# RWKV in a hybrid trunk layer: Gram products of two heads in turn, wider group spacing, other buffer counts, split weights kept in DRAM

## The chip, the core and the metric

The kernel runs on one core of a Trainium2 chip. The core has a matrix engine (TensorE, PE in the profile, with PEld for its weight loads), three engines for element work (VectorE, DVE; ScalarE, ACT; GpSimd, POOL) and a queue engine (SyncE, SP) that issues the transfers between DRAM and the on-chip memory. The engines run side by side, each in the order of its own instruction list, and wait for each other through semaphores. Matrix products land in PSUM, eight banks of 128 partitions by 512 fp32 numbers; everything else on chip is in SBUF. The metric is the device time of one execution in microseconds.

## What is computed

One layer over 2048 positions of width 1024. The normalised input goes through one input projection (1024 to 4224 columns), whose columns feed three groups: an RWKV-7 group of eight heads of 64, an S5 group and an RG-LRU group. Each group's output is gated; the concatenation goes through an output projection, and a per-layer embedding is added. Cut to what matters here:

```python
xn = rmsnorm(h, norm_g)
zin = xn @ w_in                          # 1024 x 4224
z_rw, g_rw, u_s5, g_s5, x_lru, g_lru = jnp.split(zin, SPLITS, axis=-1)
# RWKV: token shift, decay d, kk = k / |k|, b = kk * a, and per head
def step(S, inp):
    r_t, k_t, v_t, kk_t, b_t, d_t = inp
    S = S * d_t - (S kk_t) b_t^T + v_t k_t^T
    return S, S r_t
y = group_norm(y) * ln_w + ln_b + bonus;  y_rw = y * silu(g_rw)
h = h + concat(y_rw, y_s5, y_lru) @ w_out
h = h + rmsnorm(p @ ple_w) * sigmoid(h @ ple_gate_w)
out = rmsnorm(h)
```

## The kernel before

**Stages.** First comes one long stretch with the input projection, RWKV and RG-LRU; then the S5 group with the first output products between its steps (`o1a`), then S5's gating (`glu`), then the embedding and the end (`stage_a`, `stage_b`). The first stretch works on two halves of 1024 positions, each in two blocks of 512.

**Projection (`fills`).** 33 panels of 128 columns of `w_in`. `fetch_w` loads a panel as two pieces of 256 KB; `split_w` (L188) writes it as a rounded part `whi` (ACT, L192) and the rest `wlo` (DVE, L193, by the helper at L80), two buffers each; `inproj` (L327) runs 24 products per block: `whi` and `wlo` with the rounded input, `whi` with the input's rest. Both halves load and split all panels. `more()` starts the next panel whenever one is taken. In front of each half, `load_xn` transposes the normalised input rows on TensorE (L319); the rows of the second half are loaded into SBUF buffers that RWKV uses too (`XT`, among them `bk`, `ms`, `kb` and `gr`).

**RWKV.** 16 units, each two head pairs' worth of 256 positions in eight chunks of 64; partitions 0 to 63 hold one head, 64 to 127 the other. Each unit goes through three stages:

- `rwkv_front` (L376): decay and scaling; `kx` (queries and keys, three sets of columns), `bk`; then the Gram products of keys with queries (L461), for each half of the chunks and each head four products of 64 rows by 128 columns into one PSUM bank (`pprep`, two banks, also used by others); ACT copies parts of the bank to `mt` (L466), DVE multiplies the masks into `kx` and `gr` (L468).
- `rwkv_solve` (L471): DVE solves the 32 x 32 triangular blocks in 31 steps (L484 to L489), transposes the result to `tn` and then, in four pieces of 32 partitions, into `tm` (L497); TensorE transposes `bk` into `kb` (L504); small products fill the off-diagonal block of `tm` (L530 from `mt` and `tn`, L541).
- `rwkv_chain` (L549): four steps of state recurrence with products L570, L581, L585 (reads `tm`), L592 and L603, each step three ticks; then the group norm (L608 to L619).

**Order.** TensorE's order is written by hand, by the loop at L879 to L903. Each round is a tick: the projection gets a credit of 10 (9 after the first eight units), a k-step of three products costs 3; then chain, solve and front run up to their next `yield`, whose value says after how many ticks they go on. `W_BK` is the wait between `kx`/`bk` and the Gram, `yield 1` stands before each Gram group, `W_SOLVE` = 8 stands before L530, and a front starts at least 15 ticks (`INTERVAL`) after the one before. A front waits at L428 until the unit two before it has left the chain; `kx`, `gr`, `mt` and `tm` have two buffers. The other engines' orders, and SP's, come from a planner that places each instruction by priority and by when its plan has the inputs ready; the on-chip space of a later stage is that of ended ones, and each later tile waits for the last reader of what lay there.

**After the stretch.** L976 to L981 load `w_out` in rows of 512 KB through three staging buffers (`ht`), round them on ACT (L105) and subtract on DVE; L1008 transposes a small S5 table; `o1a(0)` (L958 to L966) uses the `w_out` rows in the order in which they come.

Of the kernel before, what the change touches and what calls it, by code (L numbers as in the profile page):

```python
# [9 lines left out]
F32 = mybir.dt.float32  # L10
# [7 lines left out]
P = 128  # L18
# [4 lines left out]
C = 64  # L23
# [2 lines left out]
TU = TB // 2  # L26
CHUNK_MM, INTERVAL = (10, 9), 15
PR_C, PR_S, PR_F, PR_W = 100, 50, 0, 0
W_LOAD, W_Z, W_BK, W_SOLVE, W_GN, W_C = 2, 1, 3, 8, 1, 1
K_LATE = (3, 5)  # L30
KD = D // P
CT = W // P
# [12 lines left out]
def hymba_layer(ctx: ExitStack, tc: tile.TileContext, x, p, norm_g, w_in,  # L45
# [20 lines left out]
    Ud = dram.tile([W, T5, NC5], F32, name="Ud")  # L66
    Gd = dram.tile([CT, P, SEQ], F32, name="Gd")
    Zd = dram.tile([W, T5, NC5], F32, name="Zd")

    def pmm(bufs=3):  # L70
        return psum.tile([P, 512], F32, tag="mm", name="ps_mm", bufs=bufs)

    def pprep():
        return psum.tile([P, 512], F32, tag="prep", name="ps_prep", bufs=2)

    def plate():
        return psum.tile([P, 512], F32, tag="late", name="ps_late", bufs=1)
# [4 lines left out]
    def mul(out, a, b):  # L82
        tt(out, a, b, ALU.mult)
# [4 lines left out]
    def sub(out, a, b):  # L88
        tt(out, a, b, ALU.subtract)

    def ts(out, a, s1, op0, s2=None, op1=None):
        if op1 is None:
            V.tensor_scalar(out=out, in0=a, scalar1=s1, scalar2=None, op0=op0)  # L93
        else:
            V.tensor_scalar(out=out, in0=a, scalar1=s1, scalar2=s2, op0=op0, op1=op1)
# [89 lines left out]
            nc.sync.dma_start(out=raws[-1], in_=w_v[:, ks, c0:c0 + P])  # L185
        return raws

    def split_w(raws):  # L188
        hi = wpool.tile([P, KD, P], F32R, tag="whi", name="whi", bufs=2)
        lo = wpool.tile([P, KD, P], F32R, tag="wlo", name="wlo", bufs=2)  # L190
        for ks, raw in zip(w_halves, raws):
            A.copy(out=hi[:, ks], in_=raw)  # L192
            sub(lo[:, ks], raw, hi.bitcast(F32)[:, ks])  # L193
        return hi, lo

    rows, off = [], {}
# [179 lines left out]
    def rwkv_front(pair, z, n):  # L376
# [48 lines left out]
        nc.sync.dma_start(out=inv, in_=nd.rearrange("h b c t -> (h b c) t").unsqueeze(1).broadcast_to([32, 4, 32]))  # L425
        ts(inv, inv, 1e-24, ALU.max)
        V.reciprocal(out=inv, in_=inv)
        while len(chained) < n - 1:  # L428
            yield 0
        kx = wt("kx", [P, NCH, 3, C], 2)  # L430
        mul(kx[:, :, 2], ch(r), ep[:, :, 1:C + 1])
        mul(kx[:, :, 0], ch(kk), ep[:, :, 0:C])
        A.copy(out=kx[64:128, :, 1], in_=kx[64:128, :, 0])
# [13 lines left out]
            stt(r[:, cs], r[:, cs], col("r_k", hp), km[:, cs], ALU.mult, ALU.mult)  # L447
        yield W_BK

        gr = wt("gr", [P, NCH, 2, C], 2)  # L450
        mt = wt("mt", [P, NCH, C], 2)
        for half_c in range(2):
            yield 1
            cs = slice(4 * half_c, 4 * half_c + 4)
            for h in range(2):
                os = slice(64 * (1 - h), 64 * (1 - h) + 64)
                ps = pprep()
                for q in range(4):
                    c = 4 * half_c + q
                    hs = slice(64 * h, 64 * h + 64)  # L460
                    T.matmul(out=ps[:, q * P:(q + 1) * P], lhsT=bk[hs, c].rearrange("p a t -> p (a t)"),  # L461
                             rhs=kx[hs, c, h:3:2 - h], start=True, stop=True)
                psq4 = ps.rearrange("p (c t) -> p c t", t=P)
                for bl in range(2):
                    g = slice(64 * h + 32 * bl, 64 * h + 32 * bl + 32)
                    A.copy(out=mt[g, cs, 0:C - 32 * bl], in_=psq4[g, :, 32 * bl:C])  # L466
                for dst, rs, o in ((kx[os, cs, h], os, 0), (gr[:, cs, h], slice(0, P), C)):
                    mul(dst, psq4[rs, :, o:o + C], gm[rs, o:o + C].unsqueeze(1).broadcast_to([dst.shape[0], 4, C]))  # L468
        return kx, gr, mt, inv, bk, r, dl

    def rwkv_solve(n, v, mt, inv, bk, r):  # L471
        def wt(tag, shape=None, bufs=1):
            return pool_of(tag).tile(shape, F32, tag=tag, name=tag, bufs=bufs)
# [8 lines left out]
        for o, n in ((0, 16), (16, 15)):  # L482
            mul(ms[:, o:o + n, o + 1:32], ms[:, o:o + n, o + 1:32], inv[:, o + 1:32].unsqueeze(1).broadcast_to([P, n, 31 - o]))
        for st in range(31):  # L484
            ni, n = st // 4 + 1, 31 - st
            tmp = wt("stmp", [P, 8, 32], 2)
            mul(tmp[:, 0:ni, 0:n], xs[:, 0:ni, st:st + 1].broadcast_to([P, ni, n]),
                ms[:, st:st + 1, st + 1:32].broadcast_to([P, ni, n]))
            sub(xs[:, 0:ni, st + 1:32], xs[:, 0:ni, st + 1:32], tmp[:, 0:ni, 0:n])  # L489
        tn = wt("stmp", [P, 8, 32], 2).rearrange("p i (c q) -> p i c q", q=4)  # L490
        V.transpose(out=tn.rearrange("p i c q -> p i (c q)"), in_=xs)
        tm = wt("tm", [P, NCH, C], 2)
        for h in range(2):
            G.memset(tm[64 * h + 32:64 * h + 64, :, 0:32], 0.0)
            for bl in range(2):
                g = slice(64 * h + 32 * bl, 64 * h + 32 * bl + 32)
                V.transpose(out=tm[g, :, 32 * bl:32 * bl + 32], in_=tn[g].rearrange("p i c q -> p c i q"))  # L497

        kb = wt("kb", [P, NCH, P], 2)
        for q in range(2):  # L500
# [26 lines left out]
        for c in range(NCH):  # L527
            for h in range(2):
                o = 64 * h
                T.matmul(out=psc[o + 32:o + 64, 32 * c:32 * c + 32], lhsT=mt[o:o + 32, c, 32:64],  # L530
                         rhs=tn[o:o + 32, :, c], start=True, stop=True, tile_position=(o, o + 32))
        qn = wt("stmp", [P, 8, 32], 2)
        for h in range(2):
            hs = slice(64 * h + 32, 64 * h + 64)
            A.copy(out=qn[hs], in_=psc[hs, 0:256].rearrange("p (c t) -> p c t", t=32))
        yield 1
        psd = plate()
        for c in range(NCH):
            for h in range(2):
# [9 lines left out]
    def rwkv_chain(pair, half, q, q_, gd):  # L549
# [15 lines left out]
        for st in range(NS):  # L565
# [162 lines left out]
    def fills(half, xt, w, prev):  # L728
# [7 lines left out]
        raws, ws = [w], []  # L736
# [91 lines left out]
    fronts, begun, solved, chained, ended = [], [], [], [], []  # L828

    def need(*key):  # L830
        while key not in done:
# [301 lines left out]
    def wt(tag, shape, bufs=1):  # L1133
        return sw.tile(shape, F32, tag=tag, name=tag, bufs=bufs)
# [280 lines left out]
```

## Time and profile before

| what | us |
|---|---|
| median of three runs | 1819.96 |
| the three runs | 1819.87 to 1821.08 |
| the profiled execution, its own time | 1823.06 |
| its span, first to last instruction | 1821.3 |
| TensorE busy in the span | 1747.5 |
| VectorE busy | 1287.9 |
| ScalarE busy | 968.8 |

The stretch with RWKV and the projection runs from the start to about 1157 us. In the rows of a stretch, "(x3624)" is the number of instructions, and the clock column is the share of TensorE's full clock that was granted (0.989 over the span). A row of a timeline begins with its start and its length in us; "[4.99 <-DMA st]" says that the engine stood idle for 4.99 us before it and what ended that. Rows with the same line in sequence are merged, with their count. A row of a group ends with total busy us and the mean of one in ns, then the idle time before such instructions. Every fp32 product stands as two rows in the trace (512 rows at L461 for 256 products), a transpose as one.

### The profile page before, as it was taken

How to read it: one execution, taken by the hardware profiler on the slowest of the kernel's cores; microseconds unless marked ns; L12 is line 12 of the kernel's file. 1: busy time of each engine (PE TensorE's matmuls, PEld its weight loads, DVE VectorE, ACT ScalarE, POOL GpSimd, SP SyncE). 2: the span in 40 equal slices, each digit the busy share in tenths (PEclk: the TensorE clock that was granted, in tenths of full speed). 3: DMA queues.
4: the chain of work that ended last, by engine and by line, in shares of the span. 5: the costliest groups of instructions: out<-in, count | busy, mean ns of one | idle time of the engine just before them, and what ended most of it. 6: DMA issues, size and time to landing. Idle time of an engine off the chain costs nothing. (4 is left out here: it accounts for less than half of the span.)

```text
span 1821.3 us, 30173 instructions
## 1 busy us (share of the span) xinstructions
PE 1747.5 (96%) x11212; PEld 1346.6 (74%) x11212; DVE 1287.9 (71%) x3219; ACT 968.8 (53%) x1857; POOL 43.7 (2%) x105
## 2 busy tenths in 40 slices
PE   5999999999998999999999999899999999999997
PEld 4877777777676777777776767678888778888886
DVE  6279788688887439888688885786875685555554
ACT  5345864575757445665558565666763452232222
POOL 1000000000000000000000000000000000000000
PEclk9999999999999999999999999999999999999999
DMA  4332323222223233123222121742334893223220
GB/s 147 116 108 79 93 78 99 90 61 77 83 71 100 82 116 112 52 86 101 82 80 67 51 69 38 197 142 98 110 105 119 221 311 143 85 92 110 78 73 35
DMA packets 214620, 184.71 MB, mean 101 GB/s; under 512 B 59253, under 2 KB 182474, under 8 KB 214474
## 3 DMA queue, kind: packets, MB, share of 16 engines
q1 hardware_dynamic: 214474, 182.79, 32.5%
q8 instruction: 88, 1.44, 0.3%
q14 instruction: 58, 0.48, 0.1%
HBM read 121.73 MB, written 59.83 MB: 100 GB/s over the span
## 5 line engine op out<-in xcount | busy, mean ns | idle before, releaser
L332 PE MATMUL ps_mm<-xh,whi 128*128 128x512 f32 x1056 | 463.0, 438 | 0.9 <-ACT whi L192 0.7
L333 PE MATMUL ps_mm<-xh,wlo 128*128 128x512 f32 x1056 | 416.3, 394 | 0.8 <-DVE wlo L80 0.8
L334 PE MATMUL ps_mm<-xl,whi 128*128 128x512 f32 x1056 | 416.5, 394 | 0.0
L332 PEld LDWEIGHTS ps_mm<-xh,whi 128*128 128x128 f32 x1056 | 200.0, 189 | 79.1 <-issue 31.3
L333 PEld LDWEIGHTS ps_mm<-xh,wlo 128*128 128x128 f32 x1056 | 200.6, 190 | 46.6 <-issue 13.0
L334 PEld LDWEIGHTS ps_mm<-xl,whi 128*128 128x128 f32 x1056 | 200.0, 189 | 45.2
L80 DVE TENSOR_TENSOR stmp<-xs,ms 128x60 f32<-128x60 f32 (+24 forms) x496 | 103.3, 208 | 11.6
L80 DVE TENSOR_TENSOR xs<-xs,stmp 128x60 f32<-128x60 f32 (+24 forms) x496 | 102.7, 207 | 11.5
L923 PE MATMUL ps_mm<-woh,yl 128*128 128x512 f32 x256 | 103.1, 403 | 2.0 <-DVE yl L98 2.0
L922 PE MATMUL ps_mm<-woh,yh 128*128 128x512 f32 x256 | 102.4, 402 | 0.5 <-ACT yh L101 0.4
L924 PE MATMUL ps_mm<-pgl,hh 128*128 128x512 f32 x256 | 101.1, 395 | 0.3 <-DVE pgl L80 0.3
L924 PE MATMUL ps_mm<-wol,yh 128*128 128x512 f32 x256 | 101.3, 396 | 0.0
L923 PE MATMUL ps_mm<-pgh,hl 128*128 128x512 f32 x256 | 101.0, 394 | 0.0
L922 PE MATMUL ps_mm<-pgh,hh 128*128 128x512 f32 x256 | 100.8, 394 | 0.0
L80 DVE TENSOR_TENSOR wlo<-wraw,whi 128x512 fp32r<-128x512 f32 x132 | 88.5, 683 | 14.0 <-ACT whi L192 13.6
L101 ACT ACT_TABLE_LOAD x74 | 94.9, 1283 | 1.3
L101 ACT ACTIVATE ftg<-ps_mm 128x512 f32<-128x512 f32 x32 | 19.1, 598 | 135.4 <-PE ps_mm L924 135.4
L98 DVE SCALAR_TENSOR_TENSOR z<-ps_mm,pc,z 128x511 f32<-128x511 f32 x48 | 35.8, 745 | 69.9 <-ACT z L101 69.8
L192 ACT CAST whi<-wraw 128x512 fp32r<-128x512 f32 x132 | 77.9, 614 | 0.7 <-DMA wraw<-in_w_in 0.2
L98 DVE SCALAR_TENSOR_TENSOR e<-ftg,e 128x1024 f32<-128x1024 f32 x16 | 19.6, 1226 | 78.1 <-ACT ftg L101 78.1
L101 ACT ACTIVATE uv<-ps_chain 64x128 f32<-64x128 f32 x64 | 17.4, 272 | 97.9 <-DVE uv L93 97.2
L101 ACT ACTIVATE z<-ps_mm,dc 128x512 f32<-128x512 f32 x48 | 32.8, 682 | 66.3 <-PE ps_mm L334 66.2
(332 smaller groups left out, 3535.9 us busy)
## 6 DMA issues: line engine op xcount, KB each, us to landing
wraw<-in_w_in SPq DMA_DIRECT2D x132, 256.0 KB
zd<-z SPq DMA_DIRECT2D x48, 256.0 KB
yr<-Yd SPq DMA_DIRECT2D x16, 512.0 KB
Hd<-ht SPq DMA_DIRECT2D x16, 512.0 KB
hr<-Hd SPq DMA_DIRECT2D x16, 512.0 KB
xr<-in_x SPq DMA_DIRECT2D x16, 512.0 KB
out<-e SPq DMA_DIRECT2D x16, 512.0 KB
st<-in_w_out SPq DMA_DIRECT2D x12, 512.0 KB
```

What stands on the lines that cost most here:

```text
L80: V.tensor_tensor(out=out, in0=a, in1=b, op=op)
L98: V.scalar_tensor_tensor(out=out, in0=a, scalar=s, in1=b, op0=op0, op1=op1)
L101: A.activation(out=out, in_=in_, func=func, scale=scale, bias=bias)
L192: A.copy(out=hi[:, ks], in_=raw)
L332: T.matmul(out=ps, lhsT=hi[:, k], rhs=xh, start=(k == 0), stop=False)
L333: T.matmul(out=ps, lhsT=lo[:, k], rhs=xh, start=False, stop=False)
L334: T.matmul(out=ps, lhsT=hi[:, k], rhs=xl, start=False, stop=(k == KD - 1))
L922: T.matmul(out=ps, lhsT=a_h[:, k], rhs=b_h[k][:, ns], start=(ends[0] and k == 0), stop=False)
L923: T.matmul(out=ps, lhsT=a_l[:, k], rhs=b_h[k][:, ns], start=False, stop=False)
L924: T.matmul(out=ps, lhsT=a_h[:, k], rhs=b_l[k][:, ns], start=False, stop=(ends[1] and k == nk - 1))
```

## The change

- **Gram.** The two heads' products are issued in turn, chunk by chunk, into two banks taken together, and both banks are read afterwards. The first group comes one tick after the wait, the second three ticks after the first (`W_GR`); `W_BK` goes from 3 to 4.
- **Waits of the order.** `kx` has three buffers, and the front waits for the chain of three units before it there; before the Gram it waits for the chain of two units before it and for L530 of the unit before (`coupled`). `mt` and `tm` have one buffer; L541's products wait in the order until the last L585 of the unit before is issued (`used`).
- **Transposes into `tm`.** Two of 128 partitions instead of four of 32; the two memsets of POOL that zero a block come after them.
- **Weights.** In the first half `split_w` also stores both parts of each panel to DRAM (`Wd`); in the second half `load_w` loads these into the `whi` and `wlo` buffers, and nothing is fetched or split there.

```diff
-W_LOAD, W_Z, W_BK, W_SOLVE, W_GN, W_C = 2, 1, 3, 8, 1, 1
+W_LOAD, W_Z, W_BK, W_GR, W_SOLVE, W_GN, W_C = 2, 1, 4, (1, 3), 8, 1, 1
+    Wd = dram.tile([w_in.shape[2] // P, 2, P, KD, P], F32, name="Wd")
...
+    def load_w(j):
+
+        pair = w_pair()
+        for i, part in enumerate(pair):
+            nc.sync.dma_start(out=part.bitcast(F32), in_=Wd[j, i])
+        return pair
...
             sub(lo[:, ks], raw, hi.bitcast(F32)[:, ks])
+        for i, part in enumerate((hi, lo)):
+            nc.sync.dma_start(out=Wd[j, i], in_=part.bitcast(F32))
         return hi, lo
...
-        while len(chained) < n - 1:
+        while len(chained) < n - 2:
             yield 0
-        kx = wt("kx", [P, NCH, 3, C], 2)
+        kx = wt("kx", [P, NCH, 3, C], 3)
...
+        while len(chained) < n - 1 or len(coupled) < n:
+            yield 0
         gr = wt("gr", [P, NCH, 2, C], 2)
-        mt = wt("mt", [P, NCH, C], 2)
+        mt = wt("mt", [P, NCH, C])
         for half_c in range(2):
-            yield 1
+            yield W_GR[half_c]
             cs = slice(4 * half_c, 4 * half_c + 4)
+            pair_ps = [pprep(), pprep()]
+
+            for q in range(4):
+                c = 4 * half_c + q
+                for h in range(2):
+                    hs = slice(64 * h, 64 * h + 64)
+                    T.matmul(out=pair_ps[h][:, q * P:(q + 1) * P], lhsT=bk[hs, c].rearrange("p a t -> p (a t)"),
+                             rhs=kx[hs, c, h:3:2 - h], start=True, stop=True)
             for h in range(2):
                 os = slice(64 * (1 - h), 64 * (1 - h) + 64)
-                ps = pprep()
-                for q in range(4):
...
-                psq4 = ps.rearrange("p (c t) -> p c t", t=P)
+                psq4 = pair_ps[h].rearrange("p (c t) -> p c t", t=P)
...
-        tm = wt("tm", [P, NCH, C], 2)
+
+        tm = wt("tm", [P, NCH, C])
+        for bl in range(2):
+            V.transpose(out=tm[:, :, 32 * bl:32 * bl + 32], in_=tn.rearrange("p i c q -> p c i q"))
         for h in range(2):
             G.memset(tm[64 * h + 32:64 * h + 64, :, 0:32], 0.0)
-            for bl in range(2):
-                g = slice(64 * h + 32 * bl, 64 * h + 32 * bl + 32)
-                V.transpose(out=tm[g, :, 32 * bl:32 * bl + 32], in_=tn[g].rearrange("p i c q -> p c i q"))
...
+        coupled.append(0)
         qn = wt("stmp", [P, 8, 32], 2)
...
         yield 1
+        while len(used) < n:
+            yield 0
         psd = plate()
...
+            if st + 1 == NS:
+                used.append(0)
             ts(uv[heads[0], cs, 0], ps[heads[0], 1], -1.0, ALU.mult)
...
         def more():
+            if half > 0:
+                j = next(begun_w, None)
+                if j is not None:
+                    ws.append(load_w(j))
+                return
             if raws:
-                ws.append(split_w(raws.pop(0)))
+                ws.append(split_w(raws.pop(0), next(begun_w)))
...
-                w = fetch_w(O_LORA)
+                w = None
```

The solve's loops rename a variable as well (`n` to `w`), so that `n` stays the unit's number where `used` is compared.

More of the change, by code (lines that the diff above doesn't have):

```diff
@@ L186, in fetch_w, with w_pair, split_w @@
         return raws
-    def split_w(raws):
-        hi = wpool.tile([P, KD, P], F32R, tag="whi", name="whi", bufs=2)
-        lo = wpool.tile([P, KD, P], F32R, tag="wlo", name="wlo", bufs=2)
+    def w_pair():
+        return [wpool.tile([P, KD, P], F32R, tag=tag, name=tag, bufs=2) for tag in ("whi", "wlo")]
+    def load_w(j):
[3 more added lines that the diff above has]
+        return pair
+    def split_w(raws, j):
+        hi, lo = w_pair()
         for ks, raw in zip(w_halves, raws):
@@ L448, in rwkv_front @@
         yield W_BK
+        while len(chained) < n - 1 or len(coupled) < n:
+            yield 0
         gr = wt("gr", [P, NCH, 2, C], 2)
-        mt = wt("mt", [P, NCH, C], 2)
+        mt = wt("mt", [P, NCH, C])
         for half_c in range(2):
-            yield 1
+            yield W_GR[half_c]
             cs = slice(4 * half_c, 4 * half_c + 4)
+            pair_ps = [pprep(), pprep()]
[5 more added lines that the diff above has]
+                             rhs=kx[hs, c, h:3:2 - h], start=True, stop=True)
             for h in range(2):
                 os = slice(64 * (1 - h), 64 * (1 - h) + 64)
-                ps = pprep()
-                for q in range(4):
[L459 to L462, printed above, removed]
-                psq4 = ps.rearrange("p (c t) -> p c t", t=P)
+                psq4 = pair_ps[h].rearrange("p (c t) -> p c t", t=P)
                 for bl in range(2):
@@ L481, in rwkv_solve @@
         mul(xs, xi0, inv.unsqueeze(1).broadcast_to([P, 8, 32]))
-        for o, n in ((0, 16), (16, 15)):
-            mul(ms[:, o:o + n, o + 1:32], ms[:, o:o + n, o + 1:32], inv[:, o + 1:32].unsqueeze(1).broadcast_to([P, n, 31 - o]))
+        for o, w in ((0, 16), (16, 15)):
+            mul(ms[:, o:o + w, o + 1:32], ms[:, o:o + w, o + 1:32], inv[:, o + 1:32].unsqueeze(1).broadcast_to([P, w, 31 - o]))
         for st in range(31):
-            ni, n = st // 4 + 1, 31 - st
+            ni, w = st // 4 + 1, 31 - st
             tmp = wt("stmp", [P, 8, 32], 2)
-            mul(tmp[:, 0:ni, 0:n], xs[:, 0:ni, st:st + 1].broadcast_to([P, ni, n]),
-                ms[:, st:st + 1, st + 1:32].broadcast_to([P, ni, n]))
-            sub(xs[:, 0:ni, st + 1:32], xs[:, 0:ni, st + 1:32], tmp[:, 0:ni, 0:n])
+            mul(tmp[:, 0:ni, 0:w], xs[:, 0:ni, st:st + 1].broadcast_to([P, ni, w]),
+                ms[:, st:st + 1, st + 1:32].broadcast_to([P, ni, w]))
+            sub(xs[:, 0:ni, st + 1:32], xs[:, 0:ni, st + 1:32], tmp[:, 0:ni, 0:w])
         tn = wt("stmp", [P, 8, 32], 2).rearrange("p i (c q) -> p i c q", q=4)
         V.transpose(out=tn.rearrange("p i c q -> p i (c q)"), in_=xs)
-        tm = wt("tm", [P, NCH, C], 2)
+        tm = wt("tm", [P, NCH, C])
+        for bl in range(2):
+            V.transpose(out=tm[:, :, 32 * bl:32 * bl + 32], in_=tn.rearrange("p i c q -> p c i q"))
         for h in range(2):
             G.memset(tm[64 * h + 32:64 * h + 64, :, 0:32], 0.0)
-            for bl in range(2):
-                g = slice(64 * h + 32 * bl, 64 * h + 32 * bl + 32)
-                V.transpose(out=tm[g, :, 32 * bl:32 * bl + 32], in_=tn[g].rearrange("p i c q -> p c i q"))
         kb = wt("kb", [P, NCH, P], 2)
@@ L735, in fills @@
         jobs = iter(jobs)
-        raws, ws = [w], []
+        raws, ws, begun_w = [w], [], iter(range(w_in.shape[2] // P))
         def more():
+            if half > 0:
[3 more added lines that the diff above has]
+                return
             if raws:
-                ws.append(split_w(raws.pop(0)))
+                ws.append(split_w(raws.pop(0), next(begun_w)))
             c0 = next(jobs, None)
@@ L827, in hymba_layer @@
     units = [(half, u // 4, u % 4) for half in range(NH) for u in range(8)]
-    fronts, begun, solved, chained, ended = [], [], [], [], []
+    fronts, begun, solved, chained, ended, coupled, used = [], [], [], [], [], [], []
     def need(*key):
```

## The prediction

> **What bounds the kernel now.** I read the page first, then the busy time by stretch, then TensorE's waits in the RWKV stretch, where all edits lie.
>
> ```profile
> span 1821.3 us, 30173 instructions
> PE 1747.5 (96%) x11212; PEld 1346.6 (74%) x11212; DVE 1287.9 (71%) x3219; ACT 968.8 (53%) x1857; POOL 43.7 (2%) x105
> ...
> 100.00:570.00 470.00, 459.81 (x3624) 339.44 (x3620) 388.28 (x1158) 296.53 (x600) 7.58 (x20) 0.99 0.28 85
> 600.00:1150.00 550.00, 537.34 (x4139) 399.00 (x4138) 410.21 (x1187) 325.38 (x655) 4.28 (x14) 0.99 0.27 80
> ```
>
> The two lower rows are the two halves of the sequence (length; busy PE, PEld, DVE, ACT, POOL; clock; DMA share; GB/s). TensorE is busy 98% in both, and its order is written by hand, so what leaves it there leaves the time, unless a wait appears. DVE is next: 388.3 of 470, so 81.7 us of slack over the half's eight units, 10.2 us a unit.
>
> ```profile
> PE ps_prep L461 <- DVE gr L80: 2.5, 1, 2.5
> PE ps_y L581 <- DVE rst L80: 2.4, 3, 1.4
> PE ps_chain L592 <- ACT uv L101: 1.7, 3, 0.7
> PE ps_late L541 <- DVE tm L497: 1.3, 1, 1.3
> ...
> PE ps_mm L333 <- DVE wlo L80: 0.8, 1, 0.8
> PE ps_mm L332 <- ACT whi L192: 0.7, 1, 0.7
> ```
>
> These are TensorE's waits in the second half (us in total, times, longest): the shown rows add to 9.4 us, about all that better cover could return there.
>
> **Gram products (the term that decides).** An fp32 product is two rows of the trace, so a group of one head (four products) is eight and a pair of groups sixteen.
>
> ```profile
> L461 PE MATMUL ps_prep<-kx,bk x512: 271/272/422, 113.6 to 1063.0; 64*128 64x128 f32 x171
> ...
> 113.60 1.71 PE L461 MATMUL ps_prep<-kx,bk 64*128 64x128 f32 x16
> 115.24 0.50 PE L332 MATMUL ps_mm<-xh,whi 128*128 128x512 f32 x1
> ...
> 1058.46 1.16 PE L461 MATMUL ps_prep<-kx,bk 64*128 64x128 f32 x8
> 1062.14 1.13 PE L461 MATMUL ps_prep<-kx,bk 64*128 64x128 f32 x8 [2.52 <-DVE gr L80]
> ...
> 99.58 0.48 PE L396 MATMUL ps_prep<-zl,wla 64*128 64x256 f32 x1
> 99.59 0.48 PE L398 MATMUL ps_prep<-zl,wla 64*128 64x256 f32 x1
> 99.90 0.38 PE L396 MATMUL ps_prep<-zl,wla 64*128 64x256 f32 x1
> 99.91 0.38 PE L398 MATMUL ps_prep<-zl,wla 64*128 64x256 f32 x1
> ```
>
> Both heads take 1.71 us, one alone 1.16 and 1.13: the second head adds only 0.55, so the two already overlap in part. L396 and L398 have the same form (64 rows by 128 columns, two row halves, two banks), and there the halves start 0.01 us apart and repeat every 0.21 to 0.32 us side by side. They are queued two products, two products; the Gram is queued four and four, and the second half starts late. Alternating, it should look like L396/L398: both heads in the time of one, 1.16 + 0.01. Saved: 1.71 - 1.17 = 0.54 us a pair, 16 units times two pairs: 32 x 0.54 = **17.3 us**. Ends: 0 (no more overlap than now) and 32 x 0.55 = 17.6; I take 17.3, by the nearest rows.
>
> The Trainium skill, "TensorE: Matmul & The Clock Gate" (Part 3, What overlaps and what doesn't), says matmuls start and end in strict program order. By that rule sixteen rows would be serial now and the gain larger (the fourth rival); the interleaved rows of L396 and L398, queued two after two, do not agree with it.
>
> Could issue limit the alternating rows? The densest group of small products:
>
> ```profile
> 173.31 1.15 PE L519 MATMUL ps_late<-cen,zv 64*64 64x64 f32 x32
> ```
>
> 32 rows in 1.15 us is 36 ns each; sixteen need 0.58 of the 0.9 us that they have.
>
> **Group spacing, W_BK, the new waits.** They add no instruction; they move the order. I walked the loop by its yields. Before, kx of front n waits for chain n-2's end, and from one kx to that chain's end it is 4 + 1 + 1 + 13 + 1 + 12 = 32 ticks (bk, groups, solve, chain) for two units. After, the Gram of front n waits for solve n-1's L530 products: 1 + 3 + 1 to the next solve and 11 to its L530, 16 ticks a unit. The mean is 16 in both, so nothing in steady state. The three ticks between groups remove the 2.5 us wait above and W_BK 4 gives kx and bk longer: -3 us; ends 0 and -9.4.
>
> **DVE and ACT work.**
>
> ```profile
> L497 DVE STREAM_TRANSPOSE tm<-stmp 32x256 f32<-32x256 f32 x64 | 27.8, 435 | 1.2
> L80 DVE TENSOR_TENSOR wlo<-wraw,whi 128x512 fp32r<-128x512 f32 x132 | 88.5, 683 | 14.0 <-ACT whi L192 13.6
> L192 ACT CAST whi<-wraw 128x512 fp32r<-128x512 f32 x132 | 77.9, 614 | 0.7 <-DMA wraw<-in_w_in 0.2
> L491 DVE STREAM_TRANSPOSE stmp<-xs 128x256 f32<-128x256 f32 x16 | 7.1, 444 | 0.4
> ```
>
> Two transposes of 128 partitions at 444 ns (L491's row) for four of 435: 0.85 us less a unit. POOL's memsets now follow them; they end ticks before L585 reads tm. Kept weights remove 66 casts (40.5 us of ACT) and 66 subtractions (45.1 us of DVE) in the second half. All of it lies beside a busy TensorE, so only its waits on whi and wlo, 1.5 us, come back: **-1.5**; ends 0 and, with the three rows from L581 to L541 that wait behind other DVE and ACT work, -7.
>
> **DMA.** The first half adds 66 stores of 512 KB; the second exchanges 66 loads of 256 KB for 66 of 512 KB. DMA engines are busy 28%, so bandwidth is free. Each store stands in SP's queue until its ACT or DVE half is done, and the next raw fetch stands behind it; that fetch waits for the same split, so its place hides the store's. 66 issues at 0.41 us (two in 0.82, tail rows) are 27 us of SP; a quarter of it in front of a late fetch would be +7. I take +1; ends 0 and +7. In the second half a load waits for the panel before last; 48 products at 0.23 us, 11 us, cover its landing (3.5 us for 512 KB, tail rows; two of them 7). Behind it on SP stand z loads and spills, which have several ticks. If a landing took longer than 11 us, each of 33 panels would pay the rest.
>
> **Middle.** Unit 6's chain ends three ticks later against the fills, and its kb and gr hold the next half's x rows.
>
> ```profile
> 582.73 0.47 DVE L93 TENSOR_SCALAR xt<-xt,xry 128x512 f32<-128x512 f32 x1
> ...
> 591.82 0.60 PE L319 MATMUL ps_prep<-ident,xt 128*128 128x128 f32 x4
> ```
>
> There are 8.6 us between the last normalised row's end and its transposes. A tick of fills alone is 2.5 us (12.7 us for five, tail rows), so three are 7.6 and stay hidden; solve 7 starts five later and holds bk and ms: 12.7 - 8.6 = 4. I take +1; ends 0 and +4.
>
> **Tail (what is late next).** By the same count the last kx before comes at tick 307 and the last chain product at 307 + 31 = 338; after, solve 14's L530 at 313, and 1 + 3 + 1 + 13 + 1 + 11 later, 343. The fills end on 343 in both.
>
> ```profile
> 1143.56 0.40 PE L603 MATMUL ps_y<-gr,uv 128*64 128x64 f32 x8
> 1156.28 0.39 PE L334 MATMUL ps_mm<-xl,whi 128*128 128x512 f32 x1
> 1161.66 0.28 PE L1008 MATMUL ps_prep<-ident,st 32*128 32x32 f32 x1 [4.99 <-DMA st<-in_s_a_re]
> ...
> 1144.10 0.29 DVE L80 TENSOR_TENSOR s_carry<-sp,dl 128x128 f32<-128x128 f32 x1
> ...
> 1144.46 0.82 SPq L104 DMA_DIRECT2D st<-in_w_out  x2
> 1160.32 3.44 SPq L104 DMA_DIRECT2D st<-in_w_out  x3
> ...
> 1149.76 1.04 ACT L105 CAST woh<-st 128x1024 fp32r<-128x1024 f32 x1
> 1163.86 1.04 ACT L105 CAST woh<-st 128x1024 fp32r<-128x1024 f32 x1 [1.89 <-DMA st<-in_w_out]
> 1171.02 1.05 ACT L105 CAST woh<-st 128x1024 fp32r<-128x1024 f32 x1
> ...
> L80 DVE TENSOR_TENSOR wol<-st,woh 128x1024 fp32r<-128x1024 f32 x8 | 9.8, 1224 | 8.5 <-ACT woh L105 8.5
> ```
>
> Call F the fills' end, 1156.7. The first w_out loads leave right after the last read of sp (1144.39), 12 us before F, so eight casts run from F-7 to F+15 and o1a(0), which takes the rows as they come, stalls little beyond the 5 us of L1008. After the change only three fill products follow L603, and those loads leave at about F. A row lands in some 3.5 us (1160.32 to 1163.86), is cast in 1.04 and subtracted in 1.22; with three staging buffers one passes every 2 to 2.4 us, so the eighth is ready near F+6+7x2.4 = F+23, against F+17 now: **+6**. Ends: 0 (waits later in the stage shrink) and +12 (the whole shift).
>
> **Sum** on the profiled execution: -17.3 - 3 - 1.5 + 1 + 1 + 6 = -13.8: span 1821.3 to 1807.5. That execution's own time, 1823.06, is 1.8 us over its span; the median of the three runs is 1819.96, so the forecast is 1819.96 - 13.8 = **1806**.
>
> **Rivals.**
> *The tail eats the gain.* Mechanism as above with the full 12, and the +7 and +4 ends of stores and middle: -17.3 - 4.5 + 23 = +1: 1821. For it: the casts stand right behind the loads. Against: three ends at once. Chance 0.10.
> *Slower: one tm buffer stops DVE.* Unit n's transposes wait for chain n-1's last L585, and DVE is in order. The last L585 comes 8 ticks after the solve's start; the solve's own DVE work could end sooner if nothing else gets in:
>
> ```profile
> L80 DVE TENSOR_TENSOR stmp<-xs,ms 128x60 f32<-128x60 f32 (+24 forms) x496 | 103.3, 208 | 11.6
> L80 DVE TENSOR_TENSOR xs<-xs,stmp 128x60 f32<-128x60 f32 (+24 forms) x496 | 102.7, 207 | 11.5
> L478 DVE STREAM_TRANSPOSE ms<-mt 128x1024 f32<-128x1024 f32 x16 | 32.8, 2051 | 0.5 <-ACT mt L466 0.5
> ```
>
> That is 206/16 + 2.1 = 15 us a unit, against 8 ticks of at least 20. A stand over the 10.2 us of slack delays the copies TensorE needs. It decides beyond 10.2 + (13.8 + 3.6)/7 = 12.7 us for each of the half's seven waits; at 15 us it costs 7 x 4.8 = 34: 1840. Against: 8 ticks hold much other DVE work, and L530 reads tn, not tm. 0.10.
> *No more overlap.* The Gram stays at 1.71 and the rest moves by +3.5: 1823.5. L396/L398 speak against it. 0.06.
> *All of the Gram's length halves.* If the rows of both heads ran one behind the other now, their starts, 1.71 - 0.27 (one row's length) = 1.44 us, would shrink to half: 32 x 0.72 = 23 us, 1800. Against: the second head adds 0.55 us, less than the 0.89 that eight starts of one head take (1.16 - 0.27). 0.06. This is what the rule of the Trainium skill cited above gives.
>
> **How the numbers follow.** Forecast 0.68, its own range 1797 (waits -9.4, tail +2) to 1815 (waits 0, tail +10). 0.2% is about what a measurement of this kernel can tell from no change: 3.6 us. Faster: 0.68 + 0.06 + 0.03 of the tail case = 0.77. Same: 0.07 + 0.03 of no overlap = 0.10. Slower: 0.13. The range reaches to the tail case and just past it: 1796 to 1822, with the 1840 and the no-overlap case left out.
>
> **What would show it.** Right: L461 rows alternate, a pair takes about 1.17 us and starts of both heads lie 0.01 apart; the second-half whi row is gone; the st loads leave at the fills' end, with TensorE idle longer than 5 us or stuttering behind ACT's casts. Wrong: a pair still near 1.7 us; TensorE waits on tm or mt copies every unit; L332 waits on DMA in the second half.

## The result and the profile after

The changed kernel takes 1863.29 us (median of four runs, 1862.39 to 1869.85) against 1819.91 us (1819.26 to 1821.08) before: a ratio of 1.0233, 95% interval 1.0217 to 1.0249. It is slower by 43 us in the medians (42.4 by the ratio, as in the table further down); forecast was a gain of 14. The lines of the changed kernel bear other numbers: the Gram is L475 (L461 before), the projection L344 to L346 (L332 to L334), the first RWKV products L408 and L410 (L396, L398), their norm product L430, the bonus product L527 (L511), psc, the first off-diagonal product, L546 (L530), psd, the second, L560 (L541), and psr, the product of the group norm, L632 (L611).

First the page's head, then the two stretches of the projection, with the same columns as before.

```profile
span 1861.0 us, 30148 instructions
PE 1755.9 (94%) x11212; PEld 1342.6 (72%) x11212; DVE 1225.8 (66%) x3121; ACT 940.1 (51%) x1791; POOL 43.9 (2%) x105
```

```profile
100.00:570.00 470.00, 439.67 (x3420) 322.37 (x3416) 355.17 (x1062) 277.00 (x560) 5.93 (x17) 0.97 0.42 134
600.00:1150.00 550.00, 531.90 (x4127) 392.86 (x4128) 358.31 (x1100) 288.38 (x583) 5.43 (x17) 0.98 0.33 109
```

DVE and ACT have less to do than before (62 and 29 us), and still TensorE stands idle: in the first stretch its busy time falls from 459.8 to 439.7 us, in the second from 537.3 to 531.9. The clock falls too. Who makes it wait is in the groups of products (busy us, mean ns | idle us before them and what ended it):

```profile
L948 PE MATMUL ps_mm<-woh,yh 128*128 128x512 f32 x256 | 105.7, 415 | 10.2 <-ACT yh L102 8.4 <-ACT woh L106 1.8
...
L475 PE MATMUL ps_prep<-kx,bk 64*128 64x128 f32 x512 | 37.2, 285 | 0.0
...
L410 PE MATMUL ps_prep<-zl,wla 64*128 64x256 f32 x64 | 21.7, 467 | 9.3 <-ACT s L102 5.7 <-DVE xs L81 3.5
...
L408 PE MATMUL ps_prep<-zl,wla 64*128 64x256 f32 x64 | 19.9, 434 | 15.0 <-ACT lth L102 9.0 <-DVE stmp L81 4.4 <-DVE gr L81 1.6
...
L430 PE MATMUL ps_prep<-sq,sel 128*2 128x512 f32 x32 | 17.2, 619 | 6.1 <-DVE bon L81 5.1 <-ACT ta L102 1.1
...
L546 PE MATMUL ps_late<-stmp,mt 32*32 32x32 f32 x512 | 11.7, 197 | 18.0 <-ACT rst L102 17.9
```

Rows of the same groups before (L530, which is now L546, had no idle time there):

```profile
L922 PE MATMUL ps_mm<-woh,yh 128*128 128x512 f32 x256 | 102.4, 402 | 0.5 <-ACT yh L101 0.4
...
L461 PE MATMUL ps_prep<-kx,bk 64*128 64x128 f32 x512 | 56.4, 286 | 3.4 <-DVE gr L80 3.2 <-PE ps_late L541 0.2
...
L398 PE MATMUL ps_prep<-zl,wla 64*128 64x256 f32 x64 | 18.6, 411 | 2.9 <-DVE stmp L80 1.5 <-DVE xs L80 0.9 <-DVE bon L80 0.5
```

The Gram did what was forecast: 56.4 to 37.2 us, and its 3.4 us of waits are gone. Against that stand new waits: 24.3 us before the wla products (2.9 before), 6.1 before L430 (1.2 before L418, the same product), 18.0 before psc (none), 10.2 before L948 (0.5). Together some 54 us more. Other waits fell, so that the idle time (span less busy time) rises by 31 us in all, from 73.8 to 105.1; TensorE's busy time rises by 8 us although the Gram's fell by 19. All of the new waits but the last stand in front of a bank of PSUM that others share. Those before psc are 14 waits, one in every unit but the first of each half. How one comes about, in the timeline of TensorE and, behind it, of ACT:

```profile
335.99 1.02 PE L632 MATMUL ps_late<-rst,blk 128*128 128x512 f32 x2
339.48 0.73 PE L546 MATMUL ps_late<-stmp,mt 32*32 32x32 f32 x32 [2.47 <-ACT rst L102]
...
340.74 0.63 PE L345 MATMUL ps_mm<-xh,wlo 128*128 128x512 f32 x1
...
343.60 0.39 PE L346 MATMUL ps_mm<-xl,whi 128*128 128x512 f32 x1
```

```profile
337.45 1.28 ACT L102 ACT_TABLE_LOAD   x1
338.74 0.69 ACT L102 ACTIVATE rst<-ps_late,gneps 128x512 f32<-128x512 f32 x1
```

psr of the unit before (L632) and psc of the next (L546) follow each other with no projection product between them. Both write the one bank `ps_late`. psc may go only when ACT has read psr, and ACT loads a table first (1.28 us). TensorE, whose order is fixed, stands for 2.47 us with the projection queued behind. Then the second price: the projection's rows behind the wait take 0.63 us instead of 0.39 and start 0.43 us apart, until 343.3. Before, the two stood apart; in this unit of its timeline psr comes 5.8 us ahead of psc, and in the next, by the tick count below, as far behind it:

```profile
376.76 1.02 PE L611 MATMUL ps_late<-rst,blk 128*128 128x512 f32 x2
...
382.53 0.69 PE L530 MATMUL ps_late<-stmp,mt 32*32 32x32 f32 x32
```

The other meeting, in the two `ps_prep` banks of the changed kernel: TensorE, then DVE.

```profile
292.37 1.16 PE L475 MATMUL ps_prep<-kx,bk 64*128 64x128 f32 x16
...
297.02 1.13 PE L408 MATMUL ps_prep<-zl,wla 64*128 64x256 f32 x4
299.58 1.10 PE L410 MATMUL ps_prep<-zl,wla 64*128 64x256 f32 x4 [1.43 <-DVE xs L81]
```

```profile
295.00 2.04 DVE L494 STREAM_TRANSPOSE ms<-mt 128x1024 f32<-128x1024 f32 x1
296.89 0.38 DVE L81 TENSOR_TENSOR kx<-ps_prep,gm 64x256 f32<-64x256 f32 x1
...
299.01 0.42 DVE L81 TENSOR_TENSOR gr<-ps_prep,gm 128x256 f32<-128x256 f32 x1
```

The second Gram group has both banks from 292.4. DVE puts the 2 us transpose with which the solve begins between the reads of the two heads, then more rows of solve and chain between the second head's two reads, and is through with them at 299.4. The next unit's wla products, one tick behind the group, come at 297.0; they have the first of the banks at once and the second at 299.6. The longest of these waits (9.0 us, at 498.4) is the same with RG-LRU's work in the way: the pair is issued at 484.4, and DVE's read of the first head's bank for `gr` runs from 497.9 to 498.3.

### The profile page after: what moved, and what is told of

It reads as the page before. It is cut to its first block, busy times and chain, and to the rows that moved or that the text cites. A ratio compares the mean times of both kernels' runs of the same rounds, so it can differ in the third digit from the quotient of the medians.

```text
span 1861.0 us, 30148 instructions
## 1 busy us (share of the span) xinstructions
PE 1755.9 (94%) x11212; PEld 1342.6 (72%) x11212; DVE 1225.8 (66%) x3121; ACT 940.1 (51%) x1791; POOL 43.9 (2%) x105
## 3 DMA queue, kind: packets, MB, share of 16 engines
q8 instruction: 88, 1.44, 0.3%
## 5 line engine op out<-in xcount | busy, mean ns | idle before, releaser
L344 PE MATMUL ps_mm<-xh,whi 128*128 128x512 f32 x1056 | 462.1, 438 | 1.5 <-ACT la L102 1.5
L346 PE MATMUL ps_mm<-xl,whi 128*128 128x512 f32 x1056 | 420.3, 398 | 0.0
L344 PEld LDWEIGHTS ps_mm<-xh,whi 128*128 128x128 f32 x1056 | 202.7, 192 | 78.8 <-issue 28.4
L346 PEld LDWEIGHTS ps_mm<-xl,whi 128*128 128x128 f32 x1056 | 202.5, 192 | 45.5
L948 PE MATMUL ps_mm<-woh,yh 128*128 128x512 f32 x256 | 105.7, 415 | 10.2 <-ACT yh L102 8.4
L948 PE MATMUL ps_mm<-pgh,hh 128*128 128x512 f32 x256 | 100.8, 394 | 0.0
L102 ACT ACTIVATE ftg<-ps_mm 128x512 f32<-128x512 f32 x32 | 19.2, 599 | 135.8 <-PE ps_mm L950 135.8
L102 ACT ACTIVATE uv<-ps_chain 64x128 f32<-64x128 f32 x64 | 17.5, 273 | 100.1 <-DVE uv L94 92.0
L948 PEld LDWEIGHTS ps_mm<-woh,yh 128*128 128x128 f32 x256 | 49.2, 193 | 22.3 <-ACT yh L102 9.0
L102 ACT ACTIVATE g<-ps_mm 128x512 f32<-128x512 f32 x48 | 28.6, 595 | 63.0 <-PE ps_mm L346 62.9
```

Source lines behind the costliest of these rows:

```text
L102: A.activation(out=out, in_=in_, func=func, scale=scale, bias=bias)
L344: T.matmul(out=ps, lhsT=hi[:, k], rhs=xh, start=(k == 0), stop=False)
L346: T.matmul(out=ps, lhsT=hi[:, k], rhs=xl, start=False, stop=(k == KD - 1))
L948: T.matmul(out=ps, lhsT=a_h[:, k], rhs=b_h[k][:, ns], start=(ends[0] and k == 0), stop=False)
```

## Theory, rivals and a count of ticks

The theory: the order brings the loss, because users of a shared bank that stood apart now stand on one tick or one tick apart; alternation and kept weights only gain. Walking the loop by its `yield`s gives the distances below (ticks; they are counts and hold no time; n is a unit in the middle of a half). "psr" is how far the norm's product of unit n-1 stands behind psc of unit n; "wla" how far the wla products of unit n+1 stand behind the second Gram group of unit n; "bonus" how far the same products stand behind L527 of unit n.

| kernel | psr | wla | bonus | last chain product / fills' end |
|---|---|---|---|---|
| before | +2, then -2, in turn | +3, +4 | 0, +1 | 338 / 343 |
| changed | 0 | +1 | -2 | 343 / 343 |
| wla later | 0 | +3 | 0 | 345 / 343 |
| norm later | +2 | +1 | -2 | 343 / 343 |
| both later | +2 | +3 | 0 | 345 / 343 |
| no meeting | +2 | +6 | +3 | 342 / 343 |
| no meeting, longer fills | +2 | +6 | +3 | 346 / 361 |
| period 15 | +2 | +6 | +3 | 334 / 343 |

The runs that are not listed have the order of one that is: "alternation alone" and "old order" that of before; "no kept weights", "heads in turn" and "order only" that of changed; "no meeting, order alone" that of no meeting. Near its end, "no meeting, longer fills" leaves its row: by the same count the chain is held up some ticks there, and the last unit's wla products stand at +3 and 0.

Rivals: (A) the alternation takes both banks at once and makes the waits itself; (B) the kept weights hold SP and the DMA engines up; (C) ACT and DVE are late anyhow, and the waits only move. The runs, each against the kernel before on the same chip (difference = (ratio - 1) x 1820):

| kernel | median us | ratio, 95% interval | difference |
|---|---|---|---|
| changed | 1863.29 | 1.0233 [1.0217, 1.0249] | +42.4 |
| alternation alone | 1824.34 | 1.0006 [0.9991, 1.0021] | +1.1 |
| wla later | 1844.15 | 1.0113 [1.0085, 1.0142] | +20.6 |
| norm later | 1847.86 | 1.0137 [1.0112, 1.0162] | +24.9 |
| both later | 1838.08 | 1.0080 [1.0051, 1.0108] | +14.6 |
| no kept weights | 1869.62 | 1.0251 [1.0229, 1.0272] | +45.7 |
| heads in turn | 1885.64 | 1.0344 [1.0329, 1.0360] | +62.6 |
| no meeting | 1805.62 | 0.9906 [0.9890, 0.9922] | -17.1 |
| no meeting, longer fills | 1819.52 | 0.9984 [0.9973, 0.9994] | -2.9 |
| order only | 1891.55 | 1.0380 [1.0351, 1.0409] | +69.2 |
| no meeting, order alone | 1820.07 | 0.9978 [0.9963, 0.9993] | -4.0 |
| period 15 | 1800.79 | 0.9879 [0.9856, 0.9902] | -22.0 |
| old order | 1810.75 | 0.9931 [0.9907, 0.9955] | -12.6 |

## The experiments

**Alternation alone**: the kernel before with the Gram part of the diff.

```diff
-            for h in range(2):
-                os = slice(64 * (1 - h), 64 * (1 - h) + 64)
-                ps = pprep()
-                for q in range(4):
-                    c = 4 * half_c + q
+            pair_ps = [pprep(), pprep()]
+            for q in range(4):
+                c = 4 * half_c + q
+                for h in range(2):
...
```

> The kernel before with the Gram rows of the two heads alternating in two banks, and nothing else of the change. Theory (the loss is bank users that meet in the new order; the alternation itself gains what was forecast): 1802 to 1807 us, 32 pairs with starts over 0.9 us instead of 1.44, no idle time before L408 or before the psc products beyond that of the kernel before (2.9 and 0 us in all). Rival A (alternating itself brings the loss, since both prep banks now come free late and together): 1815 or more, with idle time before the second Gram group or before the wla products of over 15 us in all.

It gains nothing. The groups stand one tick apart here, and each takes both banks. The group of the Gram, and two of them in the timeline:

```profile
L461 PE MATMUL ps_prep<-kx,bk 64*128 64x128 f32 x512 | 42.7, 294 | 12.0 <-DVE gr L80 9.2 <-DVE bk L80 2.4 <-ACT stmp L537 0.5
```

```profile
389.37 0.48 PE L461 MATMUL ps_prep<-kx,bk 64*128 64x128 f32 x2
394.08 2.04 PE L461 MATMUL ps_prep<-kx,bk 64*128 64x128 f32 x14 [4.22 <-DVE gr L80]
...
396.65 0.63 PE L333 MATMUL ps_mm<-xh,wlo 128*128 128x512 f32 x1
```

Busy time falls from 56.4 to 42.7 us, idle time rises from 3.4 to 12.0, and the longest wait (4.22 us) is followed by rows at 0.63 us. So rival A is half right: with groups a tick apart the alternation meets itself, and its 13.7 us go back as 8.6 us of waits and some 5 us of slow rows (granted clock 0.984 over the span, 0.989 before). The wla products are innocent here (3.3 us of idle time, 2.9 before).

**wla later, norm later, both later**: the changed kernel with the one distance, the other, and both set apart.

```diff
-W_LOAD, W_Z, W_BK, W_GR, W_SOLVE, W_GN, W_C = 2, 1, 4, (1, 3), 8, 1, 1
+W_LOAD, W_Z, W_BK, W_GR, W_SOLVE, W_GN, W_C = 2, 3, 4, (1, 3), 8, 1, 1
```
```diff
         act(rst, psy, AF.Square)
-        yield 1
+        yield 3
         psr = plate()
```

> The changed kernel with W_Z 3 for 1: the wla products stand three ticks after the second Gram group instead of one; the chain's last product comes two ticks later. Theory: the idle time before L408 and L410 (24.3 us) and the longer wla rows (+8.8 us) go, less some 3 us at the tail: 1832 to 1842 us. Rival B (the stores and loads of the kept weights, or another cause on SP and DMA, hold the engines back, and the bank waits are only where it shows): 1858 to 1866. Rival C (ACT and DVE are simply late after the Gram): the waits move to the psn and bon products with most of their size: 1850 or more.

> The changed kernel with the norm's psr product three ticks after the chain's last step instead of one, so that it stands two ticks behind psc and one behind psd, which share its bank, instead of on psc's tick ahead of it. Theory: the idle time before the psc products (18 us) and the longer psr row (+8.4 us) go: 1837 to 1847 us, idle before the psc products under 3 us. Rival B (kept weights): 1858 to 1866. Rival C (ACT is late): the wait moves to psr itself, behind the read of psd, with over 10 us in all: 1853 or more.

> Both shifts together (W_Z 3, psr three ticks after the chain). Theory: the two gains add, about -50 us less 3 at the tail: 1812 to 1824 us, which leaves the longer tail and the psn waits of the change above the forecast. Rival B (kept weights): above 1855. If the two are one wait seen twice (the one only hides the other): no better than the better of the two single runs, 1832 or more.

The groups of wla later, those of norm later, one of both later, and a piece of the timeline of both later:

```profile
L410 PE MATMUL ps_prep<-zl,wla 64*128 64x256 f32 x64 | 18.0, 402 | 2.8 <-DVE bon L81 2.8
...
L546 PE MATMUL ps_late<-stmp,mt 32*32 32x32 f32 x512 | 11.2, 193 | 22.1 <-ACT rst L102 18.8 <-DVE stmp L507 3.4
```

```profile
L410 PE MATMUL ps_prep<-zl,wla 64*128 64x256 f32 x64 | 20.6, 447 | 17.6 <-ACT s L102 13.2 <-DVE xs L81 4.1 <-DVE bon L81 0.3
...
L546 PE MATMUL ps_late<-stmp,mt 32*32 32x32 f32 x512 | 11.1, 192 | 1.0 <-DVE stmp L507 0.9
```

```profile
L344 PE MATMUL ps_mm<-xh,whi 128*128 128x512 f32 x1056 | 460.3, 436 | 10.5 <-ACT la L102 6.6 <-DMA whi<-Wd 3.9
```

```profile
305.26 1.02 PE L527 MATMUL ps_prep<-zr,blk 128*128 128x512 f32 x2
306.21 1.13 PE L408 MATMUL ps_prep<-zl,wla 64*128 64x256 f32 x4
307.94 1.13 PE L410 MATMUL ps_prep<-zl,wla 64*128 64x256 f32 x4 [0.60 <-DVE bon L81]
```

Each shift takes away its own wait and leaves the other: 24.3 us before wla fall to 3.3 (0.5 before L408, 2.8 before L410), 18.0 before psc fall to 1.0. That is against rivals B and C, by whose lights the waits would have stayed or moved. In time the two are worth 21.8 and 17.5 us, a little less than expected, and together 27.8, not their sum of 39. Both later missed its 1812 to 1824 us by 14. Its rows show part of why. Three ticks behind the Gram, wla stands right behind the bonus product (L527), which holds one of the same two banks: in the timeline above the second pair of halves starts 1.7 us behind the first, and over the run that costs 3.6 us of waits. More comes back elsewhere: L344 now waits 10.5 us for ACT and for the kept weights' load, where it waited 1.5, the first chain product (L589) 4.7 where it waited 0.0, and the transposes of the input rows (L331) 20.0 instead of 16.0.

**No kept weights, heads in turn, order only**: the changed kernel without one of its parts, or without all but the order.

```diff
         def more():
-            if half > 0:
-                j = next(begun_w, None)
-                if j is not None:
-                    ws.append(load_w(j))
-                return
             if raws:
                 ws.append(split_w(raws.pop(0), next(begun_w)))
...
-        for i, part in enumerate((hi, lo)):
-            nc.sync.dma_start(out=Wd[j, i], in_=part.bitcast(F32))
         return hi, lo
```
```diff
-            pair_ps = [pprep(), pprep()]
-            for q in range(4):
-                c = 4 * half_c + q
-                for h in range(2):
...
             for h in range(2):
                 os = slice(64 * (1 - h), 64 * (1 - h) + 64)
+                ps = pprep()
+                for q in range(4):
+                    c = 4 * half_c + q
```

> The changed kernel without the kept weights: both halves fetch and split w_in as before; order, buffers, alternation and transposes stay. Theory (meeting bank users make the loss, the kept weights only save 85 us of ACT and DVE work that lies beside TensorE, and 1.5 us of waits): 1860 to 1876 us, the same waits before psc and the wla products, in the second half a little longer because ACT and DVE have more to do. Rival B (the 66 stores and the larger loads cost time on SP or the DMA engines): 1852 or less.

> The changed kernel with the Gram rows queued one head after the other as before; the rest of the change stays. Theory (with three ticks between the groups the alternation earns its full gain, which the alternation alone did not because its two groups, one tick apart, wait for each other's banks): 1876 to 1886 us, pairs with starts over 1.44 us instead of 0.89, the same waits before psc and wla. Rival A (the waits at wla come from taking both prep banks at once): the banks come free one after the other, the idle time before wla falls below 12 us, and the time stays within 1855 to 1870.

> The order and the buffers of the change alone (W_BK 4, groups three ticks apart, the new waits on coupled and used, three kx, one mt, one tm), with the Gram heads in turn, four transposes and both halves split as before. Theory (the order brings the whole loss, the other parts only gain): the changed kernel without alternation, 1885.6 us, plus what the kept weights save in the run without them (6 us): 1888 to 1898 us, that is 66 to 76 over the kernel before. If the parts make the waits for each other (the alternation, or the weight traffic): 1880 or less.

All three came out within what the theory gave. The order and the buffers alone cost 69.2 us; in that order the alternation gains 20.2 (62.6 against 42.4), the kept weights 3.3, and 3.3 are left for the two-piece transposes, which had no run of their own; both of the last lie inside the intervals. Order only, where neither alternation nor kept weights exist, has waits in the same places (its L406 and L408 are the two wla lines, L408 and L410 of the changed kernel; L543 is psc, L524 the bonus product):

```profile
L408 PE MATMUL ps_prep<-zl,wla 64*128 64x256 f32 x64 | 19.8, 434 | 11.4 <-ACT s L102 6.3 <-DVE xs L81 4.7 <-DVE gr L81 0.4
...
L406 PE MATMUL ps_prep<-zl,wla 64*128 64x256 f32 x64 | 19.0, 419 | 4.8 <-DVE stmp L81 4.0 <-DVE gr L81 0.7
...
L524 PE MATMUL ps_prep<-zr,blk 128*128 128x512 f32 x32 | 17.5, 631 | 8.3 <-ACT nrow L430 8.3
...
L543 PE MATMUL ps_late<-stmp,mt 32*32 32x32 f32 x512 | 11.1, 192 | 20.8 <-ACT rst L102 17.8 <-DVE stmp L503 3.0
```

With rivals A and B absent the waits are there: both fall as causes of the loss. Where on the two prep banks the waits stand does depend on the alternation: without it wla waits 16.2 us instead of 24.3 (16.5 with heads in turn), and the norm product and the bonus product wait 17.3 instead of 6.1, so that the sum is not smaller.

**No meeting** and **no meeting, longer fills**: the changed kernel with three constants moved, and then a fourth.

```diff
-CHUNK_MM, INTERVAL = (10, 9), 15
+CHUNK_MM, INTERVAL = (10, 9), 16
...
-W_LOAD, W_Z, W_BK, W_GR, W_SOLVE, W_GN, W_C = 2, 1, 4, (1, 3), 8, 1, 1
+W_LOAD, W_Z, W_BK, W_GR, W_SOLVE, W_GN, W_C = 2, 1, 3, (1, 3), 8, 1, 1
...
         act(rst, psy, AF.Square)
-        yield 1
+        yield 3
```

In the second, `CHUNK_MM` is (10, 8).

> The changed kernel with INTERVAL 16, W_BK 3 and the norm's psr three ticks after the chain. By a count of ticks (no time in it) the period stays 16, wla then stands six ticks after the second Gram group instead of one (and never on the tick of the bon product, which it meets with W_Z 3), psr two behind psc; the chain's last product comes at tick 342, the fills' end at 343. Theory: no idle time over 4 us in all before psc, wla, psn; wla rows at 22 us as before; Gram 35 us; what is left is the tail: 1815 to 1828 us. If tick distances are not the cause, or the wait only moves on: 1835 or more, the same as with the two single shifts.

> The same with 8 instead of 9 rows of fill work a tick in the second half, so that by the count of ticks the chain's last product (346) stands 15 ticks before the fills' end (361) instead of one. Theory (the tail costs some 10 to 15 us because the loads of w_out wait for the last chain step): 1803 to 1815 us, TensorE's wait on yh and woh in the next stage under 2 us. Against it: the ticks of the second half get a ninth shorter, so if ACT and DVE do not keep up, waits of the chain come back and it is no faster than e7_no_meeting.

The first is the decisive run. Nothing is taken out and no buffer is added; three constants move, and the time falls by 59 us, from 42.4 above the kernel before to 17.1 below it, better than the 1815 expected at best:

```profile
L948 PE MATMUL ps_mm<-woh,yh 128*128 128x512 f32 x256 | 103.7, 406 | 9.9 <-ACT yh L102 9.9
...
L475 PE MATMUL ps_prep<-kx,bk 64*128 64x128 f32 x512 | 38.9, 290 | 2.6 <-DVE gr L81 2.6
...
L410 PE MATMUL ps_prep<-zl,wla 64*128 64x256 f32 x64 | 18.0, 402 | 0.0
...
L546 PE MATMUL ps_late<-stmp,mt 32*32 32x32 f32 x512 | 11.1, 192 | 0.0
```

The waits before wla (L408 has 0.0 too) and psc are gone, and one of 2.6 us before the Gram has come. The largest of those that the kernel before did not have is L948's, at the tail; smaller ones are L344's on ACT (6.7 us, 0.9 before) and the first chain product's on DVE (L589, 4.0, 1.2 before). The change moves the constants together, so what each of the three is worth is not shown. Longer fills take L948's wait away (its row has 0.0) and yet lose 14 us: in shorter ticks the waits on DVE and ACT come back (before the Gram 6.6 us instead of 2.6, before psc 3.8 instead of 0, L344 9.2 instead of 6.7, the bonus product 2.7 instead of 0, and smaller ones), and TensorE's busy time grows from 1726.2 to 1734.6 us. That was the case named against it.

**No meeting, order alone; old order; period 15.** The first is no meeting with heads in turn and both halves split; the second is the order, waits and buffers before with the rest of the change; the third spaces the units 15 ticks apart:

```diff
-W_LOAD, W_Z, W_BK, W_GR, W_SOLVE, W_GN, W_C = 2, 1, 4, (1, 3), 8, 1, 1
+W_LOAD, W_Z, W_BK, W_GR, W_SOLVE, W_GN, W_C = 2, 1, 3, (1, 2), 8, 1, 1
...
         act(rst, psy, AF.Square)
-        yield 1
+        yield 2
```

> The spread order of e7_no_meeting (INTERVAL 16, W_BK 3, psr three ticks after the chain), with the Gram heads in turn and both halves split: the order alone, without alternation and kept weights. Theory (spreading takes the loss away but wins nothing by itself; the alternation earns 17.5 us and the kept weights 6): 1805.6 + 23.5 = 1829, 1823 to 1834 us. Rival (the spread order itself is what beats the kernel before): 1818 or less.

> The order, waits and buffers of the kernel before with the change's alternation, two transposes and kept weights. Theory (with groups one tick apart the alternation gives back in waits what it saves, as measured alone; the kept weights save 6): 1812 to 1819 us. Rival (in the old order the kept weights free ACT and DVE for the Gram's copies, and the waits between the groups go): 1808 or less.

> The changed kernel with W_GR (1, 2), W_BK 3 and psr two ticks after the chain: by the count of ticks the period is 15, no two users of a bank stand on one tick, wla six ticks after the second Gram group, psr one behind psd, and the chain's last product at 334, nine ticks before the fills' end (343). Theory (the tail's 9 us wait on yh is what is left of the loss): 1793 to 1802 us, with no wait on yh over 1 us. Against it: the Gram groups stand two ticks apart and the solve has one tick less to the psc products; if that is too little, waits on gr and stmp come back: 1806 or more.

Spreading alone is worth 4.0 us against the kernel before (by the interval 1.3 to 6.7), a little better than the theory's range (which began at 1823) and not the rival's 1818: the other 13.1 us of no meeting come from alternation, kept weights and transposes. The old order with these parts gains 12.6, just below the range given. The alternation by itself gained nothing in that order and still has its waits there (10.3 us before L473), so kept weights and transposes are worth nearly 14 us in it (by the two intervals, give or take 5). In the changed order the two are worth 6.6 (69.2 against 62.6, give or take 6), so that a difference between the orders is not shown. I have no single row for the 14: the idle time before the transposes of the input rows falls from 20.7 us with the alternation alone to 17.1, and the rest is spread in pieces of some 2 us and less. What brings them stays open. Period 15 is the fastest of all, 22.0 us under the kernel before:

```profile
L948 PE MATMUL ps_mm<-woh,yh 128*128 128x512 f32 x256 | 103.1, 404 | 0.8 <-ACT yh L102 0.8
...
L613 PE MATMUL ps_chain<-uv,kb 128*64 128x64 f32 x512 | 28.9, 234 | 13.6 <-ACT uv L102 12.9
```

Its last chain product comes nine ticks ahead of the fills' end, and L948's wait is 0.8 us, as forecast. What pays for it is the chain: L613 now waits 13.6 us for ACT, where it waited 3.4.

## Why the prediction was wrong

**The step that failed** is in "Group spacing, W_BK, the new waits": "The mean is 16 in both, so nothing in steady state." The count of the period was right and answered the wrong question. With the old waits the units came in turn 14 and 18 ticks apart, with the new one all 16; what I did not lay side by side is where psr, psc, Gram, wla and the bonus product then stand to each other in the banks that they share. The tick table above would have shown 0 and +1. By the run with the order only it is worth +69.2 us against the -3 that I gave it; some 17 of them are the tail's share (the span ends 681.9 us behind the fills' end, 664.6 before). In the spread order, with the same new waits and buffers, the same measurement gives -4.0. The part of it that I did name held: the 2.5 us wait before the second Gram group went (L475 has 0.0).

**The Gram**: right in size and mechanism. The pair takes 1.16 us for 16 rows (the row at 292.37; forecast 1.17); the group fell by 19.2 us with the clock as it is, and the run with heads in turn puts the gain at 20.2 (forecast 17.3). But the term needed a condition: it holds where the groups stand far enough apart for the banks to come free. One tick apart, the same edit gave nothing. The two rivals on this term fall: the pair did not stay at 1.71 us, and its starts did not halve (1.16 less a row's 0.27 is 0.89 us, against 1.44 before).

**DVE and ACT**: no wait on whi or wlo is left in the second half, so the -1.5 is there; the kept weights gave 3.3 in all here, which is inside the intervals. **DMA**: the +1 is not to be seen; without the kept weights it is not faster. Waits on a load of `Wd` are small where they show up at all (2.3 us in wla later, 3.9 in both later, 1.4 in period 15). **Middle**: the +1 is not to be seen either; the transposes of the input rows wait 16.0 us, 20.6 before.

**The tail** was mis-sized: forecast +6, ends 0 and +12. The fills end at 1182.6 (the last L346 row, below), the span 678.4 us later; before it was 1821.3 - 1156.7 = 664.6: +13.8 us.

```profile
1182.17 0.40 PE L346 MATMUL ps_mm<-xl,whi 128*128 128x512 f32 x1
...
1193.87 1.22 PE L948 MATMUL ps_mm<-woh,yh 128*128 128x512 f32 x2 [6.56 <-ACT yh L102]
...
1196.32 0.63 PE L949 MATMUL ps_mm<-woh,yl 128*128 128x512 f32 x1
```

```profile
1183.22 1.28 ACT L102 ACT_TABLE_LOAD   x1
...
1191.81 1.04 ACT L106 CAST woh<-st 128x1024 fp32r<-128x1024 f32 x1 [1.41 <-DMA st<-in_w_out]
1192.77 1.05 ACT L102 ACTIVATE yh<-yr 128x1024 fp32r<-128x1024 f32 x1
```

I counted the rows of `w_out`, one each 2 to 2.4 us. What ends last is `yh`, the other operand, which stands in ACT's list behind the last unit's norm with its table loads and behind two casts; the second of these had itself waited 1.41 us for its row. The first output product starts 11.3 us behind the fills' end (before: 1162.02 against 1156.7, 5.3 us). That is 6 of the 13.8 us. The rest is not one wait: in all, TensorE's idle time behind the fills' end grows by 6.8 us (25.9 to 32.7) and its busy time by 7.0 (638.7 to 645.7), with rows at 0.63 us and a clock of 0.74 over the first 26 us. In period 15, where the norm is over before the fills end, the span stands 1798.5 - 1133.7 = 664.8 us behind them, the tail of before.

**The slower rival** had the right sign and the wrong mechanism: no wait on `tm` from the single buffer is among the rows, and no meeting and period 15 are faster than the kernel before with single `mt` and `tm`. What I had listed under "wrong" (a wait every unit) came at psc, but for a bank and not for `tm` or `mt`. Where nobody meets, the measured -17.1 us stand beside the forecast -13.8, but that closeness is partly luck: alternation, kept weights and transposes bring -13.1 there, where the terms for them and for the transfers add to -17.8, and the order with its tail brings -4.0, where the terms for it, the middle and the tail add to +4.

## What to carry to other kernels

Where an order is written by hand and several stages share a few banks, an edit that keeps the period but shifts the phases has to be checked bank by bank: list for each bank the ticks of all its users across neighbouring units, before and after, and price each pair that comes closer than the read between them takes. Products that use two banks at once gained 20 us here where the second group followed the first by three ticks, and nothing where it followed by one. And a delay at the end of a long stretch is to be followed down the in-order list of each engine, not only along the transfers.

## What the runs showed of the hardware

The matrix clock can fall after waits that are not long. Behind 1.83 us of idle time rows of the projection take 0.63 us until 472.8, instead of 0.39 (timeline of the changed kernel):

```profile
468.82 0.69 PE L546 MATMUL ps_late<-stmp,mt 32*32 32x32 f32 x32 [1.83 <-ACT rst L102]
...
469.82 0.63 PE L345 MATMUL ps_mm<-xh,wlo 128*128 128x512 f32 x1
...
472.81 0.55 PE L346 MATMUL ps_mm<-xl,whi 128*128 128x512 f32 x1
```

And a row of the busy time by stretch:

```profile
340.00:344.00 4.00, 4.00 (x22) 3.17 (x16) 1.56 (x3) 3.69 (x6) 0.00 (x0) 0.57 0.97 324
```

That is the stretch behind the 2.47 us wait shown at the top: TensorE is busy in all 4 us, at a clock of 0.57. A row starts 0.43 us behind the one before instead of 0.23, so each such stretch of some 3.5 us costs another 1.6 us that no wait view lists. Over the span the granted clock is 0.989 before, 0.977 in the changed kernel, 0.991 in period 15. The Trainium skill, "TensorE: Matmul & The Clock Gate" (Part 1, What's actually happening), puts half rate behind an idle window of about 3.4 us. Half rate agrees with these rows; the length does not, since 1.83 us of idle time in the trace were enough here. Nor does the length of a wait alone decide: in the same trace the clock halves behind 1.46 us of idle time (before psc, at 400.7) and stays full behind 2.44 us (before L430, at 825.5) and 1.93 us (before L410, at 989.3). Not every wait of 2 us has the second price, then, and these runs do not show what decides.
